# First half's recurrent phase of a decoder block: every engine's queue in program order, left operands four products ahead, recurrent gates one product later

## The chip, the cores and the metric

The kernel runs on one core of a Trainium2 chip. The metric is the device time of one execution in microseconds (us); lower is better. Times are medians of repeated runs. Engines are named as in the profile: PE (matrix multiplication), ACT (activations and copies), DVE and POOL (elementwise work), SP (which here only issues DMAs; ACT issues some too).

## What is computed

One layer of a decoder: a normalised input `h` goes through one wide projection `w_in`; its columns feed a recurrent branch, an attention branch and two merge gates.

```python
h = rms_norm(x, g_norm) * (1 + scale) + shift
x_rnn, z_rnn, q, k, v, z_attn, g_r, g_a = split(h @ w_in)      # 2048 x 1024 @ 1024 x 8192
xc = causal_depthwise_conv(x_rnn, conv_w, conv_b)              # 4 taps
r = sigmoid(blocks(xc) @ w_a + b_a); i = sigmoid(blocks(xc) @ w_x + b_x)
log_a = -8 * r * softplus(-lam); a = exp(log_a)
hr = scan(a, sqrt(1 - exp(2 * log_a)) * i * xc)                # h_t = a_t h_{t-1} + b_t
y_rnn = (hr * silu(z_rnn)) @ w_out_rnn
y_attn = (dilated_attention(rope(q), rope(k), v) * silu(z_attn)) @ w_out_attn
merged = sigmoid(g_r + b) * y_rnn + sigmoid(g_a + b) * y_attn
out = rms_norm(x + gate * (merged @ w_o), g_final)
```

All numbers are float32. A product of two float32 matrices is made of three matmuls on split operands: high times high, high times low, low times high (`mm3`). A split is one ACT copy (the high part, `hi_act`) and one POOL subtraction (the low part, `lo_pool`).

## The kernel before

The sequence of 2048 positions is worked on in two halves (`f` = 0 and 1), each of two column blocks of 512 (`j` = 0, 1). In each half the projection comes first; attention and the output products follow after both halves.

**One pair of weight tiles is seven products.** `strassen` multiplies a 2x2 arrangement of weight tiles with a 2x2 arrangement of `h` by Strassen's scheme: seven products instead of eight, each of 12 matmuls (four k-steps of `mm3`), into five PSUM tiles X, Z, W, V, Y. PE's order in a pair is X, the previous pair's last product, Z, W, V, X again, Y; the pair's own last product (into V again) is done after the next pair's X. After each product DVE or ACT adds partial results (`u1`, `u2`, `u3`) or totals a block (`total`) and hands it to `done`.

**Left operands.** The seven left operands of a pair are sums and differences of four raw weight tiles. In the first half `left_operands` makes them: four loads from HBM (`raw_tile`, a ring of five), sums on DVE (L255, L256, L258, L263) and a split of each into a tile S of a ring of seven (`split_s`: ACT L200, POOL L160). `first_operands` is a generator, so an operand is made where the program takes it for its product, and each is stored to a scratch tensor `sD` by a DMA on ACT's queue (L273). In the second half the operands are only loaded back from `sD`.

**The recurrent phase.** In each half 22 pairs come first: eight recurrent ones (`recurrent`, `m` = 0 to 7), each followed by one or two others (gates of the attention and merge branches in `gate_pairs`, plain parts of q and k in `plain_pairs`). That is 154 products. Per recurrent pair and column block, a chain of steps follows the pair's product X: `tap` (ACT), `taps` (three DVE operations, L779), `split` (ACT L154, POOL L160 into xh and xl), `gates` (six matmuls on PE into two PSUM tiles pg), `sigmoids` (ACT L792), `decay` (POOL, DVE L797), `exponentials` (ACT L802 to L804), `root` (DVE L808, ACT L809 square root), `scan` (DVE L814), `finish` and `store`. `steps_after` puts each step a number of products behind the start, and `run_late` runs it in the program after that product. The other half of a recurrent pair, `z_part`, has a sigmoid on ACT (L755) and a multiplication on POOL (L759).

**What sets the order.** In this part a scheduler does: the program gives instructions and their dependences, and the scheduler orders each engine's queue by its own estimate of when things will be ready. A few instructions are given priority (`tc.high_priority`). Once placed, an engine's queue is worked in that order on the chip: an instruction that waits holds up what stands behind it. The attention stage further on is already written under `tc.manual_schedule()`, where each engine's queue is in program order. After the recurrent phase come the rotated and the remaining plain pairs of q and k with their rotary tables (six pairs, 42 products), still in the scheduler's hands.

Of the kernel before, what the change touches and what calls it, by code (L numbers as in the profile page):

```python
# [26 lines left out]
H = 8  # L27
# [59 lines left out]
def decoder_block(ctx, tc, x, c, positions, g_norm, w_mod, b_mod, w_in, b_gate, conv_w, conv_b,  # L87
# [110 lines left out]
    def split_s(src):  # L198
        t = s_tile([P, 2, KH, P])
        last_hi[0] = nc.scalar.activation(t[:, 0], src, AF.Copy).ins  # L200
        lo_pool(t[:, 1], src, t[:, 0])
        return t

    pair_id, last_hi, last_load, last_lo, last_copy = {}, [None], [None], [None], [None]
# [3 lines left out]
    def run_late(n):  # L208
        for fn in (*late.pop(n, ()), *after_prod.pop(n, ())):
            fn()  # L210

# [14 lines left out]
    def blocks(pieces):  # L226

        cuts, tiles = [], ([], [])
# [17 lines left out]
        a11, a21, a22 = load(0, 0), load(1, 0), load(1, 1)  # L246
        return a11, load(0, 1), a21, a22

    def left_operands(pieces):

        a11, a12, a21, a22 = blocks(pieces)
        yield split_s(a11)
        s1 = T(wq, [P, KH, P], F32, "s1", bufs=1)
        s2 = T(wq, [P, KH, P], F32, "s2", bufs=1)
        nc.vector.tensor_tensor(s1[:], a21, a22, ALU.add)  # L255
        nc.vector.tensor_tensor(s2[:], s1[:], a11, ALU.subtract)  # L256
        yield split_s(s2[:])
        nc.vector.tensor_tensor(a21, a11, a21, ALU.subtract)  # L258
        yield split_s(a21)
        yield split_s(s1[:])  # L260
        yield split_s(a12)
        yield split_s(a22)
        nc.vector.tensor_tensor(s2[:], a12, s2[:], ALU.subtract)  # L263
        yield split_s(s2[:])

    def first_operands(x, pieces):

        for i, t in enumerate(left_operands(pieces)):
# [8 lines left out]
            yield t  # L277
# [41 lines left out]
    def strassen(up, f, key, pieces, done):  # L319

        x = pair_id.setdefault(key, len(pair_id))
        ops = None if f else first_operands(x, pieces)
        if f and x == 0:
            for _ in range(NS):
                load_next()

        def take():
            return (f, *loaded.pop(0)) if f else (f, 7 * x, next(ops))
# [397 lines left out]
    def reset_rows(rp, f):  # L726
        bigr = T(rp, [P, HALF], BF16, "bigr")
        for q in range(2):
            t = T(rp, [P, CH], I32, "sg", bufs=1)
# [4 lines left out]

    def recurrent(rp, bigr, f, m):
        raw = T(rp, [P, 2, P], F32, "gr_", bufs=1)
        nc.sync.dma_start(raw[:, 0, :], w_a[0, m])
        nc.sync.dma_start(raw[:, 1, :], w_x[0, m])
        gh = T(rp, [P, 2, P], F32R, "gh", bufs=1)
        gl = T(rp, [P, 2, P], F32R, "gl", bufs=1)  # L740
        hi_act(gh[:], raw[:])
        lo_pool(gl[:], raw[:], gh[:])
# [5 lines left out]
        def z_part(j, ps, u):  # L748
# [4 lines left out]
            def sigmoid():  # L753
                sg.append(T(rp, [P, CH], F32, "sg", bufs=1))
# [6 lines left out]
        def x_part(j, ps, u):  # L761
# [23 lines left out]
            def gates():  # L785
                for gt in range(2):
                    v["p", gt] = T(pg, [P, CH], F32, "pg")
                    mm3(v["p", gt][:], gh[:, gt, :], gl[:, gt, :], v["xh"][:], v["xl"][:])
# [17 lines left out]
            def root():  # L806
                t = v["t"][:]
                nc.vector.scalar_tensor_tensor(t, v["y"][:], 1.0, t, ALU.add, ALU.mult)  # L808
                nc.scalar.activation(t, t, AF.Sqrt)  # L809

            def scan():
# [3 lines left out]
                nc.scalar.activation(htail[:, m : m + 1], y[:, CH - 1 : CH], AF.Copy)  # L815

            def finish():
                z4 = zs[j][:].rearrange("p (r j) -> p r j", r=4)
# [15 lines left out]
        strassen(rp, f, ("r", m), [wcol(m * P), wcol(D + m * P)], done)  # L834
# [59 lines left out]
    def rotated_pairs(qp, f, Ct, St):  # L894

        for base, dstT, qs in QK:
# [15 lines left out]
            strassen(qp, f, (base, "rotated"), [wcol(base + hh * P, 32) for hh in range(H)], rotated)  # L912

    def plain_pairs(f):

        cuts = []
        for t in range(6):
            pieces = []
            i0 = t * P
            while i0 < (t + 1) * P:  # L920
                hd, i = divmod(i0, 96)
                n = min(96 - i, (t + 1) * P - i0)
                pieces.append((i0 - t * P, hd * P + 32 + i, n))
                i0 += n
            cuts.append(pieces)
        for base, dstT, qs in QK:
            for t in range(0, 6, 2):
                def plain(i, j, ps, u, t=t, dstT=dstT, qs=qs):
# [3 lines left out]
                    for p0, r0, m in cuts[t + i]:  # L932
                        nc.sync.dma_start(dstT[r0 : r0 + m, :, n * P : (n + 1) * P],
                                          t0[p0 : p0 + m, :].rearrange("p (r j) -> p r j", r=4))

                strassen(plain_pool[0], f, (base, t), [wcol(base + r0, n) for pc in cuts[t : t + 2] for _, r0, n in pc], plain)
                yield


    def gate_pairs(ep, f):  # L940
        for m in range(0, KT, 2):
            for base, dst, b0 in ((5 * D, zaT, None), (6 * D, grT, C_BG), (7 * D, gaT, C_BG + 8)):
                def gate(i, j, ps, u, m=m, dst=dst, b0=b0):
# [6 lines left out]
                    if b0 is None:  # L950
                        sg = T(ep, [P, CH], F32, "sg", bufs=1)
                        nc.scalar.activation(sg[:], v[:], AF.Sigmoid)
# [648 lines left out]
```

## Time and profile before

| | |
|---|---|
| median of 3 runs | 2337.65 us (2332.69 to 2343.75) |
| the profiled execution | 2338.7 us, its span 2336.9 us |
| PE busy | 2246.0 us, 96% of the span |
| DVE / ACT / POOL busy | 1347.5 / 1206.0 / 952.1 us |
| DMA | 569.21 MB, mean 244 GB/s |
| granted PE clock | 0.983 of full speed, mean |

In the profile a line number is one of the code above. Many instructions share a helper's line: all matmuls are L146, and a row names the tile written and those read (`V<-T,S`). PE is busy nearly all the time, so what can be won is the time in which it waits, and the time in which it runs at a lower clock. The stages by time from the span's start: values and set-up to 147.6 us, the first half's recurrent phase to about 641.5, its rotated and plain pairs to about 775, the second half to about 1455, attention and output after that.

### The profile page before, as it was taken

How to read it: one execution, taken by the hardware profiler on the slowest of the kernel's cores; microseconds unless marked ns; L12 is line 12 of the kernel's file. 1: busy time of each engine (PE TensorE's matmuls, PEld its weight loads, DVE VectorE, ACT ScalarE, POOL GpSimd, SP SyncE). 2: the span in 40 equal slices, each digit the busy share in tenths (PEclk: the TensorE clock that was granted, in tenths of full speed). 3: DMA queues.
4: the chain of work that ended last, by engine and by line, in shares of the span. 5: the costliest groups of instructions: out<-in, count | busy, mean ns of one | idle time of the engine just before them, and what ended most of it. 6: DMA issues, size and time to landing. Idle time of an engine off the chain costs nothing.

```text
span 2336.9 us, 34037 instructions
## 1 busy us (share of the span) xinstructions
PE 2246.0 (96%) x11461; PEld 1872.0 (80%) x11461; DVE 1347.5 (58%) x2442; ACT 1206.0 (52%) x2391; POOL 952.1 (41%) x734
## 2 busy tenths in 40 slices
PE   8998999899989999999999999999999898989998
PEld 4996777677777998787888877888889797978887
DVE  4737666756676534544434472366666777658443
ACT  4636656665643635555444411567768787634111
POOL 2456556665545533332211120446565656433000
PEclk9999999999999999999999999999999999999999
DMA  7375777676778759999677778989987887799532
GB/s 263 108 237 205 277 265 262 239 243 246 242 246 268 227 174 327 311 325 322 227 231 225 234 250 269 301 245 266 279 254 247 236 245 238 221 310 281 179 122 95
DMA packets 427284, 569.21 MB, mean 244 GB/s; under 512 B 71942, under 2 KB 292834, under 8 KB 426084
## 3 DMA queue, kind: packets, MB, share of 16 engines
q1 hardware_dynamic: 389268, 447.27, 62.2%
q10 hardware_dynamic: 37648, 119.70, 13.3%
q8 instruction: 91, 1.49, 0.3%
q14 instruction: 85, 0.70, 0.1%
q0 software_dynamic: 192, 0.05, 0.0%
HBM read 355.08 MB, written 211.82 MB: 243 GB/s over the span
## 4 chain that ended last, share of the span: by engine, by line
PE 50%; DMA 8%; DVE 4%; ACT 3%; issue 3%; POOL 2%; SPq 1%; ACTq 0%; POOLq 0%; DVEq 0%
PE pj L146 11%; PE pq L146 7%; PE X L146 6%; PE V L146 6%; PE o L146 4%; PE sc L146 4%; PE Z L146 3%; PE W L146 3%; PE Y L146 2%; PE pT L1217 1%; DMA wD<-s 1%; PE pT L1230 1%; PE pg L146 1%; DMA vraw<-vN 1%; DVE yl L163 1%
## 5 line engine op out<-in xcount | busy, mean ns | idle before, releaser
L146 PE MATMUL pj<-yh,S 128*128 128x512 f32 x1024 | 372.0, 408 | 6.1 <-DMA S<-wD 3.2
L146 PE MATMUL V<-T,S 128*128 128x512 f32 x1344 | 334.3, 397 | 12.0 <-ACT t L809 5.2
L160 POOL TENSOR_TENSOR S<-R,S 128x512 fp32r<-128x512 f32 x168 | 241.8, 1455 | 253.8 <-ACT S L200 79.2
L146 PE MATMUL X<-T,S 128*128 128x512 f32 x1344 | 332.4, 395 | 1.2 <-ACT t L888 1.2
L146 PEld LDWEIGHTS V<-T,S 128*128 128x128 f32 x1344 | 252.6, 189 | 75.9 <-ACT t L809 7.2
L146 PEld LDWEIGHTS X<-T,S 128*128 128x128 f32 x1344 | 252.4, 188 | 61.8 <-ACT t L888 2.1
L146 PEld LDWEIGHTS pj<-yh,S 128*128 128x128 f32 x1024 | 195.6, 191 | 44.0 <-DVE fg L1424 3.6
L146 PE MATMUL pj<-yl,S 128*128 128x512 f32 x512 | 203.0, 397 | 0.0
L1133 ACT ACTIVATE pp<-pp,st 128x256 f32<-128x256 f32 (+3 forms) x256 | 133.9, 524 | 113.4 <-DVE st L1132 112.7
L146 PE MATMUL W<-T,S 128*128 128x512 f32 x672 | 174.1, 404 | 0.0
L146 PE MATMUL Y<-T,S 128*128 128x512 f32 x672 | 168.6, 398 | 2.1 <-DVE t L418 2.1
L146 PE MATMUL Z<-T,S 128*128 128x512 f32 x672 | 167.4, 397 | 0.0
L146 PEld LDWEIGHTS W<-T,S 128*128 128x128 f32 x672 | 130.3, 194 | 32.4 <-issue 0.9
L146 PEld LDWEIGHTS Y<-T,S 128*128 128x128 f32 x672 | 127.0, 190 | 33.3 <-DVE t L418 2.5
L146 PEld LDWEIGHTS Z<-T,S 128*128 128x128 f32 x672 | 127.5, 190 | 30.2
L160 POOL TENSOR_TENSOR S<-s,S 128x512 fp32r<-128x512 f32 x84 | 114.9, 1369 | 77.7 <-ACT S L200 55.0
L163 DVE TENSOR_TENSOR ptl<-pT,pth 128x384 fp32r<-128x384 f32 (+1 forms) x160 | 97.8, 628 | 64.8 <-ACT pth L154 62.6
L1197 ACT ACTIVATE pp<-pp,M 128x256 f32<-128x256 f32 (+3 forms) x256 | 117.9, 523 | 8.7 <-DVE M L1321 8.6
L1132 DVE CUSTOM_DVE_ANT_0 pp<-sc,msk 128x256 f32<-128x256 f32 (+3 forms) x256 | 105.1, 449 | 30.0 <-PE sc L146 27.2
L779 DVE SCALAR_TENSOR_TENSOR xc<-xr,par,xc 128x512 f32<-128x512 f32 x96 | 84.8, 883 | 56.5 <-ACT xc L773 55.6
L160 POOL TENSOR_TENSOR kq<-kraw,kq 128x512 fp32r<-128x512 f32 (+1 forms) x64 | 101.1, 1590 | 22.9 <-ACT kq L154 22.9
L160 POOL TENSOR_TENSOR vh<-vraw,vh 128x256 fp32r<-128x256 f32 (+1 forms) x64 | 67.2, 1050 | 105.1 <-ACT vh L154 99.4
(358 smaller groups left out, 4697.7 us busy)
## 6 DMA issues: line engine op xcount, KB each, us to landing
sD<-S ACTq DMA_DIRECT2D x196, 512.0 KB, 4.2
S<-sD SPq DMA_DIRECT2D x196, 512.0 KB, 5.0
S<-wD SPq DMA_DIRECT2D x99, 512.0 KB, 5.5
R<-in_w_in_dram SPq DMA_DIRECT2D x136, 256.0 KB, 3.9
wD<-s ACTq DMA_DIRECT2D x64, 256.0 KB, 5.5
T<-in_w_mod_dram SPq DMA_DIRECT2D x8, 1024.0 KB, 11.5
vN<-ev SPq DMA_DIRECT2D x64, 128.0 KB, 2.7
zaT<-ev SPq DMA_DIRECT2D x32, 256.0 KB, 4.5
```

The lines of the kernel that those rows point to most:

```text
L146: last_mm[0] = nc.tensor.matmul(o, lhsT=l, rhs=r, start=st, stop=sp, **kw).ins
L160: nc.gpsimd.tensor_tensor(o, i, h.bitcast(F32), ALU.subtract)
L163: return nc.vector.tensor_tensor(o, i, h.bitcast(F32), ALU.subtract).ins
L779: nc.vector.scalar_tensor_tensor(xc, xr[:, i : i + CH], cw(i), xc, ALU.mult, ALU.add)
L1132: nc.vector.tensor_tensor_reduce(pdst, s_ps, mask, 1.0, 3e38, ALU.add, ALU.min, m_)
L1133: nc.scalar.activation(pdst, pdst, AF.Exp, bias=m_, scale=-1.0, accum_out=l_)
L1197: nc.scalar.activation(pp, pp, AF.Copy, scale=w)
L1217: nc.tensor.transpose(pt[:, c0 + j * P : c0 + (j + 1) * P], pp[i][:, k * P : (k + 1) * P], ident)
L1230: nc.tensor.transpose(pt[:, c * P : (c + 1) * P], pp[:, half * P : (half + 1) * P], ident)
```

## The change

1. In the first half the recurrent phase runs under `tc.manual_schedule()`: PE, DVE, ACT, POOL and SP each work in the order in which the program is written. The second half and the rotated pairs stay with the scheduler.
2. The left operands are no longer made when taken. `operand_events` lists each load, sum and split with the product that it belongs to; `pump`, called behind each product's late steps, does those that are due, LEAD = 4 products ahead of the product that uses them. Raw loads are 10 to 5 products ahead of their pair. `pair_order` gives the pairs in advance.
3. The recurrent steps from `gates` on are one product later (GATES = 5 for 4). The square root gets a step of its own, one product behind `root`'s DVE operation. The copy of `htail` moves from `scan` to `finish`. `finish` and `store` stay at 12.
4. The recurrent pair's weights `w_a`, `w_x` are loaded four products after the pair's start and split after seven.
5. Gate pairs: sigmoid one product after the total, the multiplication and the store up to two after. Plain pairs: the store one after. The tile `sg` has two buffers.

Points 3 to 5 hold in both halves.

```diff
     def run_late(n):
         for fn in (*late.pop(n, ()), *after_prod.pop(n, ())):
             fn()
+        pump()
...
+    LEAD = 4
+
+    def operand_events(x, pieces):
+        load, v = block_loads(pieces), {}
+        tt = nc.vector.tensor_tensor
...
+        def split(i, name):
+            first[7 * x + i] = t = split_s(v[name])
             kept.append((7 * x + i, t))
             if len(kept) > 2:
                 k, t2 = kept.pop(0)
-                with tc.issue_after(last_hi[0]):
-                    nc.scalar.dma_start(sD[k], t2[:].bitcast(F32))
+                nc.scalar.dma_start(sD[k], t2[:].bitcast(F32))
...
+        def sums():
+            for name in ("s1", "s2"):
+                v[name] = T(wq, [P, KH, P], F32, name, bufs=1)[:]
+            tt(v["s1"], v["a21"], v["a22"], ALU.add)
+            tt(v["s2"], v["s1"], v["a11"], ALU.subtract)
+
+        yield -6, lambda: raw("a11", 0, 0)
+        yield -5, lambda: raw("a21", 1, 0)
+        yield -4, lambda: raw("a22", 1, 1)
+        yield -1, lambda: raw("a12", 0, 1)
+        yield 0, sums
+        yield 0, lambda: split(0, "a11")
+        yield 1, lambda: tt(v["a21"], v["a11"], v["a21"], ALU.subtract)
+        yield 1, lambda: split(1, "s2")
+        yield 2, lambda: split(2, "a21")
+        yield 3, lambda: split(3, "s1")
+        yield 4, lambda: split(4, "a12")
+        yield 5, lambda: tt(v["s2"], v["a12"], v["s2"], ALU.subtract)
+        yield 5, lambda: split(5, "a22")
+        yield 6, lambda: split(6, "s2")
+
+    def pump():
+        while events and events[0][0] <= n_prod[0]:
+            events.pop(0)[2]()
...
+    GATES = 5
...
+        steps_after(n_prod[0], ((4, load_weights), (7, split_weights)))
...
             def root():
                 t = v["t"][:]
                 nc.vector.scalar_tensor_tensor(t, v["y"][:], 1.0, t, ALU.add, ALU.mult)
+
+            def square_root():
+                t = v["t"][:]
                 nc.scalar.activation(t, t, AF.Sqrt)
...
             steps_after(start[0] + 7 * j, (
-                (0, tap), (1, taps), (2, split), (4, gates), (5, sigmoids), (6, decay), (7, exponentials),
-                (9, root), (11, scan), (12, finish), (12, store)))
+                (0, tap), (1, taps), (2, split), (GATES, gates), (GATES + 1, sigmoids), (GATES + 2, decay),
+                (GATES + 3, exponentials), (GATES + 4, root), (GATES + 5, square_root), (GATES + 6, scan),
+                (GATES + 7, finish), (GATES + 7, store)))
...
+                    steps_after(n_prod[0], ((1, store),))
...
+                    steps_after(n_prod[0], ((1, sigmoid), (2, product)))
...
+    for x, (key, pieces) in enumerate(pair_order()):
+        pair_id[key] = x
+        events += [(7 * x + d - LEAD, len(events) + i, fn) for i, (d, fn) in enumerate(operand_events(x, pieces))]
+    events.sort(key=lambda e: e[:2])
...
+        pump()
         n = 0
-        for m in range(KT):
-            recurrent(rp, bigr, f, m)
-            for _ in range(1 + (m % 4 > 0)):
-                next(plain if n % 6 == 3 else gates)
-                n += 1
+        with nullcontext() if f else tc.manual_schedule():
+            for m in range(KT):
+                recurrent(rp, bigr, f, m)
+                for _ in range(others[m]):
+                    next(plain if is_plain(n) else gates)
+                    n += 1
```

What this does to the queues, at two places of the recurrent pair `m` = 1 in the first half. First ACT's queue before, around that pair's two z parts (sg), its conv input (xr, xc), its split (xh) and three left operands (S4, S5 and the store of S2, S3):

```order
L755 ACTIVATE sg_315_2148<-zs_311_2125 128x512
L815 ACTIVATE htail_96_499<-y_306_2100 128x1
L416 ACTIVATE xr_316_2150<-X_286_1995 128x512
L200 ACTIVATE S4_348_2317<-R3_326_2191 128x512
L273 DMA sD<-S2_341_2270 128x1024
L772 ACTIVATE xtail_95_498<-xr_316_2150 128x3
L773 ACTIVATE xc_317_2154<-xr_316_2150,par_2_61 128x512
L771 ACTIVATE xr_331_2230<-xtail_95_498 128x3
L200 ACTIVATE S5_354_2346<-R2_325_2189 128x512
L273 DMA sD<-S3_346_2295 128x1024
L755 ACTIVATE sg_330_2215<-zs_320_2177 128x512
L154 ACTIVATE xh_328_2211<-xc_317_2154 128x512
```

And the same stretch of ACT's queue in the change, from that pair's xc on (L806 is `tap`, L835 to L837 are `exponentials` of the pair before, L154 with S is a split of a left operand, L788 the z part's sigmoid):

```order
L806 ACTIVATE xc_326_2185<-xr_325_2181,par_2_61 128x512
L835 ACTIVATE t_329_2201<-y_317_2146 128x512
L836 ACT_TABLE_LOAD
L836 ACTIVATE a_328_2200<-y_317_2146 128x512
L837 ACTIVATE y_317_2146<-a_328_2200 128x512
L154 ACTIVATE gh_330_2205<-gr__311_2118 128x256
L154 ACTIVATE S3_332_2213<-s1_312_2123 128x512
L266 DMA sD<-S1_319_2151 128x1024
L154 ACTIVATE xh_336_2235<-xc_326_2185 128x512
L788 ACT_TABLE_LOAD
L788 ACTIVATE sg_338_2239<-zs_334_2219 128x512
L154 ACTIVATE S4_339_2241<-R3_305_2088 128x512
```

Before, the split xh stands behind both sigmoids of the z part; now it stands ahead of the second one, and S4 and S5 of the left operands come after it, although they belong to later products than before.

Second, PE's queue at the gates of that pair. Before:

```order
L146 MATMUL Z_332_2232<-T_157_1035,S1_335_2237 128x512
L146 MATMUL pg_336_2256<-xh_328_2211,gh_284_1991 128x512
L146 MATMUL pg_337_2260<-xh_328_2211,gh_284_1991 128x512
L146 MATMUL W_340_2268<-T_159_1037,S2_341_2270 128x512
L146 MATMUL W_340_2268<-T_160_1038,S2_341_2270 128x512
L146 MATMUL pg_336_2256<-xl_329_2213,gh_284_1991 128x512
L146 MATMUL pg_336_2256<-xh_328_2211,gl_285_1992 128x512
L146 MATMUL pg_337_2260<-xl_329_2213,gh_284_1991 128x512
L146 MATMUL pg_337_2260<-xh_328_2211,gl_285_1992 128x512
L146 MATMUL W_340_2268<-T_159_1037,S2_341_2270 128x512 x2
```

PE's queue at the same gates in the change:

```order
L146 MATMUL W_347_2291<-T_159_1037,S2_323_2175 128x512
L146 MATMUL pg_348_2307<-xh_336_2235,gh_330_2205 128x512
L146 MATMUL pg_348_2307<-xl_337_2237,gh_330_2205 128x512
L146 MATMUL pg_348_2307<-xh_336_2235,gl_331_2206 128x512
L146 MATMUL pg_349_2311<-xh_336_2235,gh_330_2205 128x512
L146 MATMUL pg_349_2311<-xl_337_2237,gh_330_2205 128x512
L146 MATMUL pg_349_2311<-xh_336_2235,gl_331_2206 128x512
L146 MATMUL V_354_2325<-T_155_1033,S3_332_2213 128x512
```

The gates moved from between Z and W, partly inside W, to behind the whole of W: one product later.

More of the change, by code (lines that the diff above doesn't have):

```diff
@@ L244, in load, with raw @@
             return t[:]
[L246 to L268, printed above, removed]
+        return load
+    LEAD = 4
+    def operand_events(x, pieces):
+        load, v = block_loads(pieces), {}
+        tt = nc.vector.tensor_tensor
+        def raw(name, i, half):
+            v[name] = load(i, half)
+        def split(i, name):
+            first[7 * x + i] = t = split_s(v[name])
             kept.append((7 * x + i, t))
@@ L325, in strassen @@
                 load_next()
+        n_op = iter(range(7 * x, 7 * x + 7))
         def take():
-            return (f, *loaded.pop(0)) if f else (f, 7 * x, next(ops))
+            if f:
+                return (f, *loaded.pop(0))
+            i = next(n_op)
+            return f, i, first.pop(i)
         def prod(ps, b, first, last, op=None):
```

116 lines of the change are left out of this document (72 added, 44 removed).

## The prediction

> **What bounds the kernel now.** I read the profile by stages first: which stage has PE time to give. This is the table of windows: the first half's recurrent phase, its rotated and plain pairs, and 400 us out of the second half.
>
> ```profile
> core 0: us, PE busy (x) PEld busy (x) DVE busy (x) ACT busy (x) POOL busy (x), PEclk, DMA share, GB/s
> 147.62:641.50 493.88, 464.92 (x1943) 369.13 (x1942) 328.14 (x342) 294.73 (x489) 300.00 (x211) 0.98 0.73 251
> 641.50:775.40 133.90, 124.47 (x536) 99.45 (x535) 88.24 (x148) 51.30 (x89) 72.55 (x53) 0.97 0.84 267
> 950.00:1350.00 400.00, 399.73 (x1717) 322.27 (x1716) 179.12 (x236) 196.51 (x302) 84.78 (x65) 1.00 0.81 268
> ```
>
> The second half is the yardstick: the same products with operands loaded back, and 1717 matmuls in 400 us are 0.233 us each, 2.80 per product. The first half's recurrent phase is 154 products of 12 matmuls and 16 gates of six, 1944 in all, so 452.9 us at that pace; it takes 493.9. **41.0 us are lost there.** The next 42 products would be 117.4 us, and 39 small transposes some 4.6 (four take about 0.47, an estimate from rows of four at 0.60 that overlap), so of 133.9 some 11.9 are lost there. The second half has nothing to give.
>
> Then the waits, for PE, in these two stages.
>
> ```profile
> PE pg L146 <- ACT xh L154: 17.0, 6, 5.8
> PE V L146 <- ACT t L809: 5.2, 5, 3.7
> PE V L146 <- DVE ev L418: 2.6, 1, 2.6
> PE pg L146 <- POOL xl L160: 2.1, 4, 0.5
> PE V L146 <- ACT S L200: 1.9, 1, 1.9
> ...
> PE pg L870 <- DVE rep L868: 5.8, 2, 5.0
> PE Y L146 <- DVE t L418: 2.1, 1, 2.1
> ```
>
> In the recurrent phase PE waits for 28.8 us; 22.2 of these are two kinds: gates that wait for the split xh (17.0), and products V named behind the square root (5.2). The other 12.2 of the 41.0 are not waits. The longest wait shows what they are, in PE's timeline:
>
> ```profile
> 215.79 1.56 PE L146 MATMUL Z<-T,S 128*128 128x512 f32 x6
> 223.17 1.22 PE L146 MATMUL pg<-xh,gh 128*128 128x512 f32 x2 [5.82 <-ACT xh L154]
> 225.04 0.64 PE L146 MATMUL pg<-xl,gh 128*128 128x512 f32 x1
> 226.33 0.63 PE L146 MATMUL pg<-xh,gl 128*128 128x512 f32 x1
> 230.12 2.96 PE L146 MATMUL V<-T,S 128*128 128x512 f32 x12
> 638.19 4.57 PE L146 MATMUL V<-T,S 128*128 128x512 f32 x12 [3.69 <-ACT t L809]
> ```
>
> After 5.82 us of waiting the next matmuls come 0.43 us apart for some 4 us, at half pace; after 3.69 us, twelve take 4.57 us instead of 2.96. So a long wait costs its length and some 2 to 3 us more, and the 12.2 go with the long waits.
>
> Why was xh late? ACT's timeline just before, then DVE's:
>
> ```profile
> 216.52 0.62 ACT L200 ACTIVATE S<-R 128x512 fp32r<-128x512 f32 x1
> 221.10 0.63 ACT L755 ACTIVATE sg<-zs 128x512 f32<-128x512 f32 x1 [3.96 <-DVE zs L418]
> 222.49 0.63 ACT L154 ACTIVATE xh<-xc 128x512 fp32r<-128x512 f32 x1 [0.76 <-DVE xc L779]
> 212.29 2.20 DVE L814 TENSOR_TENSOR_SCAN y<-a,htail,t 128x512 f32<-128x512 f32 x1
> 214.41 1.72 DVE L255 TENSOR_TENSOR s<-R,R 128x512 f32<-128x512 f32 x1
> 216.05 2.08 DVE L819 TENSOR_TENSOR zs<-y,zs 128x512 f32<-128x512 f32 x1
> 218.05 1.70 DVE L258 TENSOR_TENSOR R<-R,R 128x512 f32<-128x512 f32 x1
> 219.67 0.74 DVE L779 SCALAR_TENSOR_TENSOR xc<-xr,par,xc 128x512 f32<-128x512 f32 x1
> 220.33 0.68 DVE L418 TENSOR_TENSOR zs<-Y,u 128x512 f32<-128x512 f32 x1
> ```
>
> ACT stands for 3.96 us at a z part's sigmoid, whose input DVE totals only after 7.7 us of scan, sums and finish; xh stands behind that sigmoid, and PE's gates behind xh. No engine is full: in this stage DVE is busy 328.1 of 493.9 us, ACT 294.7, POOL 300.0. The loss is order, not load.
>
> **The change, part by part.** *Gates one later, xh ahead of the sigmoid that held it.* The taps come one product after X, the split two, the gates five. From the end of X that is five products, 14.0 us. The chain is xc 0.81 and ahead of it three small copies (some 1.0 together, an estimate), three taps 2.8, xh 0.63, xl 1.55:
>
> ```profile
> L773 ACT ACTIVATE xc<-xr,par 128x512 f32<-128x512 f32 x16 | 12.9, 805 | 0.0
> L779 DVE SCALAR_TENSOR_TENSOR xc<-xr,par,xc 128x512 f32<-128x512 f32 x48 | 44.3, 923 | 16.6 <-ACT xc L773 16.3
> L160 POOL TENSOR_TENSOR xl<-xc,xh 128x512 fp32r<-128x512 f32 x16 | 24.8, 1547 | 0.0
> L200 ACT ACTIVATE S<-R 128x512 fp32r<-128x512 f32 x87 | 53.2, 620 | 3.0 <-DMA qT<-ev 1.3 <-PE X L146 1.3 <-issue 0.2
> L160 POOL TENSOR_TENSOR S<-R,S 128x512 fp32r<-128x512 f32 x88 | 125.2, 1432 | 91.4 <-ACT S L200 61.4 <-issue 12.2 <-DVE ev L953 6.6
> L803 ACT ACT_TABLE_LOAD x16 | 20.5, 1283 | 0.1
> ```
>
> That makes 6.8 us, so 7.2 are left for queues. The 5.82 us wait fits into them: minus 17.0.
>
> *Operands four products ahead.* 11.2 us, of which a split needs 0.62 and 1.43. The remaining 9.1 cover any single wait of ACT in this stage (the longest at L755 is 5.8 us, row below). Minus 5.2, the wait of V. The square root, one product behind its DVE operation, adds to this cover.
>
> With both kinds the 12.2 of half pace go: 17.0 + 5.2 + 12.2 = 34.4 us. *What I keep* is the 6.6 us of the three small kinds (2.6 + 2.1 + 1.9): ordinary lateness of an eviction, an xl or a split. The lead may remove them too (minus 6.6), or a fixed order may add as many (plus 6.6).
>
> *Added work.* ACT's queue in the changed program has 12 more table loads in this stage and 13 more in the second half's. By the L803 row that is 15.4 and 16.7 us of ACT time, beside 294.7 of some 460 and 196.5 of 400 busy: off PE's path in both, price 0. Without that cover it would be all of 32 us. DVE, POOL, PE and the bytes moved stay the same.
>
> *Queues that a step is moved past.* Stores of gates, z and plain tiles now stand in SP's queue ahead of raw loads of later pairs, and wait there for DVE or ACT. A sum needs its last raw tile four products after that load's place in the program, 11.2 us; a load lands in 4.3:
>
> ```profile
> R<-in_w_in_dram SPq DMA_DIRECT2D x67, 256.0 KB, 4.3
> ```
>
> So 6.9 us are left for SP's waits: price 0. *The second half*: its gates, stores and sigmoids also move, but PE is busy 399.73 of 400 and its operands are seven tiles ahead; 0, and 3 at most. *Rotated pairs*: the scheduler orders them anew. The rotary tables now start on DVE some five products later, and PE's transposes stand after some 16 products instead of 11, so the 5.8 us wait for rep may shrink or grow; I take 0, between minus 6 and plus 6.
>
> Sum against the profiled execution: 2338.7 - 34.4 = 2304.3. That execution is 1.05 us above the median of 2337.65, so **2303 us** is forecast for the median, 1.5% less.
>
> **Rivals.** The waits of other engines that could take PE's place:
>
> ```profile
> ACT sg L755 <- DVE zs L418: 44.5, 11, 5.8
> DVE s L256 <- POOL S L160: 47.1, 19, 3.9
> DVE s L255 <- DMA R<-in_w_in_dram: 21.2, 6, 6.4
> DVE s L263 <- DMA R<-in_w_in_dram: 16.1, 8, 3.8
> ```
>
> *A, a part stays: DVE behind POOL.* The sum s2 overwrites the tile whose last split POOL does one product earlier, so in program order DVE still waits there (47.1 us, 2.5 each) with the totals of W and V behind it. PE's next use of V's bank is at least two products away, 5.6 us, so most is hidden. If a third reaches PE, 15.7 us come back: 2319.
>
> *B, no change: raw loads on a strict SP queue.* If stores hold the loads longer than the 6.9 us, DVE's waits for raw tiles (37.3 us) reach PE, since DVE can no longer do something else first: 2303 + 37 = 2340. Against it: the loads are issued up to ten products ahead of their pair.
>
> *C, slower: ACT falls behind the lead.* In three successive products ACT gets, per recurrent block with gates beside it, tanh 0.63, load 1.28, exp 0.63, square 0.62, load 1.28, sigmoid 0.63, split 0.62; split and sigmoid 1.25; load, square root, load, sigmoid and split 4.45: 11.4 us where three products take 8.4. These durations are ACT's rows L200, L803 and, for one activation, these:
>
> ```profile
> 205.78 0.63 ACT L802 ACTIVATE t<-y 128x512 f32<-128x512 f32 x1 [0.50 <-DVE y L797]
> 206.42 1.28 ACT L803 ACT_TABLE_LOAD   x1
> 207.72 0.63 ACT L803 ACTIVATE a<-y 128x512 f32<-128x512 f32 x1
> ```
>
> ACT is 3.0 us late after each such pile. If each reached PE, 16 times 3.0 and 1.6 of half pace (the 3.69 us wait: 4.57 against 2.96) would be 74 us: 2377. It decides from the point at which ACT's lateness passes the 9.1 us of the lead. Against it: ACT is idle a third of the stage, so piles do not add up.
>
> The Trainium skill (ScalarE: Activation LUTs, "What ACT_TABLE_LOAD costs") speaks against the change here: it gives some 1.28 us for a load and 1.38 for a drain, 2.66 for every switch. By that, an estimate, a pile would be 5.5 us longer, 8.5 behind, close to the whole lead, and rival C would gain. The trace does not bear it out: 207.72 - 206.42 is 1.30 us from the load's start to the next activation, and the load begins 0.64 after the tanh, so I give it no chance of its own.
>
> **How the numbers follow.** Forecast (2290 to 2312) 0.66; A (2312 to 2326) 0.14; B and other ways to no change 0.10; C 0.10. The low end is all of the 41.0 gone and 6 in the rotated pairs: 2337.65 - 47.0 = 2290.7, so 2290. The high end takes in A with the rotated pairs 6 worse: 2326. Outside are B and C, 0.2. A measurement of this kernel tells about 0.5%, 11.7 us, from no change: faster is below 2326, 0.80; within 0.10; slower 0.10.
>
> **What would show it.** In the changed profile: the recurrent phase ends some 34 us earlier; PE's waits for xh and for L809's successor are gone; matmul counts per 50 us are about 214 and the clock 1.0 from 150 to 600; ACT's waits at the z sigmoids may stay without PE behind them. The forecast is wrong if PE waits for S (C), if DVE waits for R and PE for DVE (B), if PE's waits for V behind DVE pass 10 us (A), or if the gain is lost again between the end of the phase and the second half.

## The result and the profile after

The changed kernel takes **2305.83 us**, median of 5 runs (2302.90 to 2308.77), beside 2335.00 us of the kernel before on the same chip: a ratio of 0.9857, 95% interval 0.9842 to 0.9873. The forecast was 2303 us. The profiled execution took 2306.3 us, with a span of 2304.5.

The table of windows of the kernel before, cut at the five stages that hold products: the first half's recurrent phase, its rotated and plain pairs, the second half's values, its recurrent phase, its rotated and plain pairs. The cuts are where the trace's products reach 154 and 196 in each half.

```profile
147.62:641.74 494.12, 465.16 (x1943) 369.33 (x1942) 328.38 (x342) 294.96 (x489) 300.00 (x211) 0.98 0.73 251
641.74:781.54 139.80, 130.37 (x576) 104.85 (x575) 92.19 (x153) 52.51 (x91) 76.66 (x56) 0.97 0.85 271
781.54:875.19 93.65, 93.04 (x783) 92.63 (x781) 42.29 (x78) 48.12 (x85) 37.29 (x26) 1.00 0.55 166
875.19:1331.48 456.29, 454.37 (x1944) 365.85 (x1943) 206.07 (x255) 234.19 (x365) 110.27 (x85) 1.00 0.82 274
1331.48:1456.73 125.25, 122.48 (x528) 96.61 (x527) 57.28 (x105) 18.63 (x32) 17.75 (x12) 1.00 0.83 270
```

The same five stages of the changed kernel:

```profile
147.81:599.79 451.98, 451.98 (x1949) 366.55 (x1947) 323.46 (x339) 310.60 (x496) 310.55 (x211) 1.00 0.79 271
599.79:745.04 145.25, 130.87 (x572) 103.77 (x571) 90.24 (x156) 55.79 (x95) 77.19 (x56) 0.96 0.82 268
745.04:842.28 97.24, 94.61 (x783) 94.19 (x781) 44.50 (x78) 49.95 (x87) 40.29 (x26) 0.98 0.52 155
842.28:1298.75 456.47, 452.06 (x1944) 365.11 (x1943) 198.62 (x254) 249.42 (x376) 109.32 (x85) 1.00 0.82 273
1298.75:1424.52 125.77, 122.70 (x529) 96.71 (x527) 58.32 (x107) 19.25 (x34) 17.73 (x12) 1.00 0.83 270
```

In the first row PE's busy time now equals the stage: 451.98 of 451.98 us at clock 1.00, against 465.16 of 494.12 at 0.98. The phase is 42.1 us shorter. The other rows give part of it back: 5.4 in the rotated and plain pairs, 3.6 in the second half's values, 0.2 and 0.5 after that. What follows the last product takes 880.0 us instead of 880.2, what precedes the first 0.2 more. -42.1 + 5.4 + 3.6 + 0.7 is the 32.4 us by which the span is shorter. The cut at 641.74 lies 0.9 us ahead of the end of the 154th product, 642.60; cut there, the first two figures are -43.0 and +6.3.

PE's waits in the recurrent phase (147 to 600 us) are gone; the table of waits names none. In the rotated pairs (600 to 745 us) they are these:

```profile
PE Z L146 <- ACT S L154: 4.5, 1, 4.5
PE pg L907 <- DVE rep L905: 3.5, 3, 1.3
PE X L146 <- ACT t L925: 2.1, 1, 2.1
PE X L146 <- ACT S L154: 1.9, 1, 1.9
PE V L146 <- DVE t L440: 1.4, 2, 1.1
```

The wait for rep fell from 5.8 to 3.5; four others are new or larger. That stage's order is still the scheduler's.

Now the place at which PE stood for 5.82 us before, the gates of the recurrent pair with `m` = 1. PE's timeline after, from the pair's second X product (200.75) to its gates, with the next pair's first and second X (206.34 and 221.65); then ACT's from the copy of the first of these X on:

```profile
200.75 2.96 PE L146 MATMUL X<-T,S 128*128 128x512 f32 x12
...
206.34 2.94 PE L146 MATMUL X<-T,S 128*128 128x512 f32 x12
...
217.48 0.39 PE L146 MATMUL pg<-xh,gh 128*128 128x512 f32 x1
...
221.65 2.96 PE L146 MATMUL X<-T,S 128*128 128x512 f32 x12
```

```profile
203.74 0.60 ACT L438 ACTIVATE xr<-X 128x512 f32<-128x512 f32 x1 [0.66 <-PE X L146]
...
209.23 0.61 ACT L154 ACTIVATE xh<-xc 128x512 fp32r<-128x512 f32 x1
...
211.15 0.63 ACT L788 ACTIVATE sg<-zs 128x512 f32<-128x512 f32 x1
...
215.69 0.60 ACT L373 ACTIVATE u<-X 128x512 f32<-128x512 f32 x1 [0.40 <-POOL S L160]
```

ACT copies the X of 200.75 out at 203.74, 0.03 us after its modelled end, and had waited 0.66 for it. xh follows at 209.23, ahead of the sigmoid at 211.15, and ends 7.6 us before the gates at 217.48. The copy u at 215.69 is of the next pair's first X, into whose bank PE adds at 221.65; experiment 4 comes back to it.

In the kernel before, the same X (PE's row) and its copy (ACT's row) lay much further apart:

```profile
202.75 2.96 PE L146 MATMUL X<-T,S 128*128 128x512 f32 x12
...
214.63 0.58 ACT L416 ACTIVATE xr<-X 128x512 f32<-128x512 f32 x1
```

That is 8.9 us from the end of X to the copy; a square root, a sigmoid and their table loads stood ahead of it in ACT's queue. Of the eight such copies of the phase, seven came 2.6 to 9.1 us after their X before the change; after it, none comes more than 0.9 us behind.

### The profile page after: what moved, and what is told of

Same layout as the page of the kernel before. It is cut to its first block, busy times and chain, and to the rows that moved or that the text cites. A ratio compares the mean times of both kernels' runs of the same rounds, so it can differ in the third digit from the quotient of the medians.

```text
span 2304.5 us, 34059 instructions
## 1 busy us (share of the span) xinstructions
PE 2230.6 (97%) x11461; PEld 1867.7 (81%) x11461; DVE 1333.6 (58%) x2442; ACT 1242.3 (54%) x2416; POOL 964.6 (42%) x734
## 4 chain that ended last, share of the span: by engine, by line
PE 55%; DMA 8%; DVE 4%; ACT 3%; issue 2%; SPq 2%; POOL 1%; ACTq 0%; POOLq 0%; DVEq 0%
PE pj L146 12%; PE pq L146 8%; PE X L146 8%; PE V L146 7%; PE sc L146 4%; PE o L146 4%; PE Z L146 4%; PE W L146 4%; PE Y L146 3%; DMA wD<-s 1%; PE pT L1299 1%; DMA S<-sD 1%; PE pT L1312 1%; PE pg L146 1%; DMA gaT<-ev 1%
## 5 line engine op out<-in xcount | busy, mean ns | idle before, releaser
L160 POOL TENSOR_TENSOR S<-R,S 128x512 fp32r<-128x512 f32 x168 | 251.8, 1510 | 189.6 <-ACT S L154 66.7
L160 POOL TENSOR_TENSOR S<-s,S 128x512 fp32r<-128x512 f32 x84 | 125.9, 1499 | 122.8 <-ACT S L154 96.4
L146 PE MATMUL W<-T,S 128*128 128x512 f32 x672 | 166.0, 395 | 0.3 <-POOL S L160 0.3
L812 DVE SCALAR_TENSOR_TENSOR xc<-xr,par,xc 128x512 f32<-128x512 f32 x96 | 92.6, 964 | 78.6 <-ACT xc L806 76.9
L154 ACT ACTIVATE S<-R 128x512 fp32r<-128x512 f32 x168 | 102.3, 623 | 58.6 <-DMA R<-in_w_in_dram 28.2
## 6 DMA issues: line engine op xcount, KB each, us to landing
T<-in_w_mod_dram SPq DMA_DIRECT2D x8, 1024.0 KB, 11.6
```

The costliest lines, as they stand in the source:

```text
L146: last_mm[0] = nc.tensor.matmul(o, lhsT=l, rhs=r, start=st, stop=sp, **kw).ins
L154: nc.scalar.activation(o, i, AF.Copy)
L160: nc.gpsimd.tensor_tensor(o, i, h.bitcast(F32), ALU.subtract)
L812: nc.vector.scalar_tensor_tensor(xc, xr[:, i : i + CH], cw(i), xc, ALU.mult, ALU.add)
```

## The experiments

My theory was that the lost time is order: waits caused by what stands ahead in a queue, and half pace behind the long ones. The rivals were the steps alone (lead and later gates, in whichever order) and load (ACT's added work). All kernels are the changed one with the edit shown. Stage times are read as above, from one profiled execution each; the changed kernel's own five spans lie between 2301.1 and 2307.0 us, so a stage is known to about 3 us, except where PE waits for nothing. Not tried: what points 4 and 5 of the change are worth in the first half, and which engine's queue has to be in program order.

**1. The scheduler's order, with the changed steps.**

```
-        with nullcontext() if f else tc.manual_schedule():
+        with nullcontext():
```

> The changed kernel, with the first half's recurrent phase left to the scheduler again; operands four ahead and gates five after X are kept in the code. Theory 1, the fixed order carries the gain, and the lead only makes that order workable: the scheduler puts instructions where its own model has them ready, waits of PE for xh or S come back, and at least half of the 41 us of the recurrent phase with them: 2320 to 2335 us. Theory 2, the lead and the later gates carry it, whoever sets the order: within 6 us of the changed kernel, 2300 to 2312 us, and the recurrent phase of 154 products takes 453 to 459 us. I hold theory 1 the likelier, 6 to 4.

Measured: 2362.32 us, ratio 1.0085 (1.0068 to 1.0103): 56.5 us slower than the changed kernel by the medians, 53 by the ratios, and slower than before. The recurrent phase takes 505.9 us. PE's two largest waits in it:

```profile
PE pg L146 <- ACT xh L154: 15.3, 6, 5.8
PE V L146 <- DVE ev L440: 14.7, 6, 6.3
```

The longest one for xh, in PE's timeline, and what stood ahead of xh on ACT and on DVE:

```profile
460.26 2.95 PE L146 MATMUL Y<-T,S 128*128 128x512 f32 x12
480.13 1.22 PE L146 MATMUL pg<-xh,gh 128*128 128x512 f32 x2 [5.77 <-ACT xh L154]
```

```profile
468.44 1.28 ACT L845 ACT_TABLE_LOAD   x1
469.74 0.63 ACT L845 ACTIVATE t<-t 128x512 f32<-128x512 f32 x1
470.28 0.58 ACT L438 ACTIVATE xr<-X 128x512 f32<-128x512 f32 x1
...
479.45 0.63 ACT L154 ACTIVATE xh<-xc 128x512 fp32r<-128x512 f32 x1 [0.29 <-DVE xc L812]
```

```profile
472.40 1.72 DVE L274 TENSOR_TENSOR s<-R,R 128x512 f32<-128x512 f32 x1
474.04 2.06 DVE L855 TENSOR_TENSOR zs<-y,zs 128x512 f32<-128x512 f32 x1
476.02 0.75 DVE L812 SCALAR_TENSOR_TENSOR xc<-xr,par,xc 128x512 f32<-128x512 f32 x1
```

PE ends this X where Y starts, near 460.3; ACT copies it out only at 470.28, behind a sigmoid, a square root and their table loads. In the changed kernel this step came 0.03 us after the X shown above. DVE then does a sum and a `finish` ahead of the taps. Same steps, same lead, same gates: theory 1 holds, and by more than its range (2320 to 2335); the steps alone are worth less than nothing (505.9 against 494.1 before).

**2. Gates at four, in the fixed order.**

```
-    GATES = 5
+    GATES = 4
```

> The changed kernel, with the gates of the recurrent block four products after X again, and all steps behind them one earlier; fixed order and lead are kept. From the end of X that leaves 11.2 us for a chain of 6.8 us, so 4.4 for queues. Theory 1, what held xh was the sigmoid ahead of it in ACT's queue, and the fixed order has removed that: PE's waits for xh stay under 3 us in sum, 2304 to 2310 us. Theory 2, the later gates carry it: the 17.0 us of waits for xh come back with half pace behind them, 8 to 26 us, 2314 to 2332 us. I hold theory 1 the likelier, 6 to 4.

Measured: 2315.78 us, ratio 0.9896 (0.9880 to 0.9913); the interval lies above that of the changed kernel. The phase takes 464.1 us, with these two waits ahead:

```profile
PE pg L146 <- POOL xl L160: 3.8, 5, 0.9
PE pg L146 <- ACT xh L154: 3.0, 3, 2.0
```

The time lies in theory 2's range, the waits nearer to theory 1: of the 17.0 us for xh only 3.0 return, so most were taken by the order; but one product less costs 12.1 us of phase, so the later gates are needed for the rest.

**3. Operands one and two products ahead** (the second kernel has 2 in the line shown).

```
-    LEAD = 4
+    LEAD = 1
```

> The changed kernel, with the left operands made one product ahead instead of four; fixed order and gates at five are kept. One product is 2.8 us, of which a split needs 2.05, so 0.7 us are left for queues. Theory 1, in a fixed order the lead is what covers ACT's piles (3.0 us behind after each, 16 of them): PE waits for S at each pile and at sums that DVE makes late, at least 16 times 3.0 and 1.6 of half pace, 74 us, so 2370 us or more. Theory 2, the fixed order alone does it and the lead is spare: 2300 to 2312 us. Theory 1 is the likelier, 8 to 2.

> The changed kernel, with the operands two products ahead instead of four. Two products are 5.6 us, of which a split needs 2.05, so 3.5 us are left for queues, and ACT is some 3.0 us behind after a pile. Theory 1, the cover has only to pass the pile: almost no waits of PE for S, the recurrent phase takes 452 to 458 us, 2303 to 2312 us. Theory 2, waits of several engines add up (POOL behind ACT, DVE behind POOL), so the cover has to be about three times the pile, as with four products: the phase takes 465 to 510 us, 2318 to 2365 us. With one product ahead it took 564.8 us. Even chances.

With one, 2418.28 us, ratio 1.0330 (1.0313 to 1.0347), and a phase of 564.8 us; with two, 2313.48 us, ratio 0.9896 (0.9876 to 0.9917), and a phase of 452.0. PE's waits with one product, in the phase:

```profile
PE X L146 <- POOL S L160: 32.1, 21, 3.2
PE X L146 <- ACT S L154: 31.3, 15, 2.9
```

PE waits at the first X of 21 of the 22 pairs. In the 15 where ACT is named, the split stands in ACT's queue behind the exponentials of that product and their table load; in the others POOL's half of the split is late. Two products pass it entirely: the phase is as short as with four, with no wait of PE in the table up to its end. Theory 1 holds in both for the phase; with two the total is 1.5 us over its range. (The 7 us over the changed kernel lie outside the phase: 2.2 ahead of the first product, 2.8 in the rotated pairs, 2.2 from there to the second half's last product.) So the fixed order alone does not do it: with one product of lead it is slower than the kernel before. Some lead is a condition; beyond two products, more of it gains nothing in this phase.

**4. More table loads,** four and eight ahead of each square root (the second kernel has 8 in the line shown).

```
+    pad = T(cp, [P, 1], F32, "pad")
...
             def square_root():
                 t = v["t"][:]
+                for i in range(4 if not f else 0):
+                    nc.scalar.activation(pad[:], ones[:], AF.Sigmoid if i % 2 else AF.Sqrt)
                 nc.scalar.activation(t, t, AF.Sqrt)
```

> The changed kernel, with four activations of one column ahead of each square root of the first half, two of them sigmoids, so that four more table loads stand in each of ACT's 16 piles there: 4 times 1.28 and 0.2, 5.9 us each, 95 us of ACT in all. ACT is then 8.9 us behind after each pile, against a lead that covers 9.1. Theory 1, the price of a load is 0 so long as the lateness stays under the lead: PE's waits in the recurrent phase stay under 10 us, and the time within 10 us of the changed kernel, 2300 to 2316 us. Theory 2, ACT's added work reaches PE in proportion (its sum is 295 and 41 busy already): half or more of the 95 us comes through, 2350 us or more. 7 to 3 for theory 1.

> The same with eight such activations and eight more table loads in each of the 16 piles: 11.9 us each, 190 us of ACT in all. ACT is then 14.9 us behind after each pile, 5.8 beyond the 9.1 that the lead covers. Theory 1, what is beyond the lead reaches PE, with half pace behind it: 16 times 5.8 and some 2, 125 us, so 2400 to 2460 us, and PE's waits are for S from ACT or POOL. Theory 2, ACT's idle third takes it up between the piles: under 2350 us. 7 to 3 for theory 1.

With four, 2383.86 us, ratio 1.0197 (1.0176 to 1.0219), phase 522.1 us. With eight, 2474.96 us, ratio 1.0587 (1.0566 to 1.0609), phase 615.9. In the windows of the phase ACT is busy 396.4 and 491.6 us, 85.8 and 181.0 more than in the changed kernel (the sixteenth square root falls behind its end, but its added activations ran directly behind the fifteenth, inside), and 70.1 and 163.9 us of these come through: the kernel with four loads goes as theory 2 says, the one with eight beyond the range of theory 1. And the waits are not for S at all. In the phase, with four loads and with eight:

```profile
PE X L146 <- ACT u L373: 40.4, 11, 5.6
```

```profile
PE X L146 <- ACT u L373: 125.8, 15, 12.3
```

The first of them, with four loads, on ACT and on PE:

```profile
217.16 1.28 ACT L847 ACT_TABLE_LOAD   x1
218.45 0.20 ACT L847 ACTIVATE pad<-ones 128x1 f32<-128x1 f32 x1
218.67 1.28 ACT L847 ACT_TABLE_LOAD   x1
...
224.51 0.63 ACT L848 ACTIVATE t<-t 128x512 f32<-128x512 f32 x1
...
226.09 0.58 ACT L373 ACTIVATE u<-X 128x512 f32<-128x512 f32 x1
```

```profile
206.91 2.97 PE L146 MATMUL X<-T,S 128*128 128x512 f32 x12
...
220.43 2.97 PE L146 MATMUL V<-T,S 128*128 128x512 f32 x12
226.71 5.49 PE L146 MATMUL X<-T,S 128*128 128x512 f32 x12 [3.31 <-ACT u L373]
```

The second X product of a pair adds into the bank from which ACT must first copy u1. That copy stands behind the root's pile; the lead of the operands does nothing for it. In the changed kernel u ended at 216.29 and that X began at 221.65: 5.4 us are the cover that decides here, not the 9.1 that I named. It is not the smallest: over the 22 pairs of the changed phase this margin is 3.2 to 8.0 us, least at the u of 258.24, whose X begins at 262.07. And ACT enters this pile 4.3 us later than in the changed kernel (15.9 us after the pair's X at 201.29, there 11.6 after the X at 200.75), so some lateness is carried on from the pile before; by which way is not shown, as ACT stood for 3.07 and 1.17 us in between, waiting for DVE. The rest of what came through is half pace, as in the X above, 5.49 us for 12 matmuls: PE's waits and the 2 us or so behind each.

**5. The second half's steps as before.** The late steps of the second half are put back (`steps_after` with the old lags where `f` is 1; those of the recurrent weights and of the plain stores, not shown, likewise); the first half is unchanged.

```
-                    steps_after(n_prod[0], ((1, sigmoid), (2, product)))
+                    steps_after(n_prod[0], ((0, sigmoid), (0, product)) if f else ((1, sigmoid), (2, product)))
...
+            if f:
+                steps_after(start[0] + 7 * j, (
+                    (0, tap), (1, taps), (2, split), (4, gates), (5, sigmoids), (6, decay), (7, exponentials),
+                    (9, root), (9, square_root), (11, scan), (12, finish), (12, store)))
+                return
```

> The changed kernel, with the second half's steps as they were before the change: gates four after X, root and square root together, sigmoid, product and stores of gate and plain pairs at once, recurrent weights loaded and split at the block's start. The first half is the changed one. In the changed kernel the second half lost 4.2 us that it did not lose before. Theory 1, the moved steps of the second half cost them, by waits of V and Z and by transfers that fall together: the span gets 3 to 5 us shorter, and from the marker of W at the first half's end to the first output product it takes again 666 us: 2300 to 2303 us. Theory 2, the scheduler's order there is different for another reason and such losses come and go: 2304 to 2308 us. 6 to 4 for theory 1.

Measured: 2307.40 us, ratio 0.9853 (0.9839 to 0.9868), the same as the changed kernel. The second half's recurrent phase takes 454.2 us, its rotated pairs 128.9, the values before them 95.7: theory 2. Together that is within 1 us of the changed kernel's 679.5, so the moved steps cost the second half nothing that can be measured.

**6. The fixed order through the rotated pairs.** The order is kept on until the last plain pair; angles, tables and the normalisation of x become late steps.

```
+            steps_after(n_prod[0], ((1, angles), *((d, lambda q=q, k=k: table(q, k))
+                                                   for d, q, k in ((2, 1, 0), (3, 1, 1), (4, 0, 0), (5, 0, 1)))))
...
+            steps_after(n_prod[0], ((18, lambda: norm_x(xp, x0)),))
...
+                steps_after(n_prod[0], ((0 if f else 1, finish),))
```

> The changed kernel, with the fixed order kept on through the first half's rotated and plain pairs: the rotary angles are written one product after the recurrent phase, the four tables two to five products after it, the normalisation of the next rows of x 18 products after it, and the last sum and the stores of a rotated tile one product after the rest. In the changed kernel these 42 products take 145.3 us, against 117.4 at full pace and some 4.6 for the transposes. Theory 1, what is lost there (23 us) is order as well, left to the scheduler: the stage takes 125 to 135 us, 2286 to 2297 us in all. Theory 2, it is load (raw tiles in 32-column pieces, rotary work on DVE, DMA share 0.93 and more): the stage stays within 4 us of 145, 2301 to 2311 us. Theory 3, in a fixed order PE stands at the transposes until DVE has made the tables: 150 us and more, over 2311 us. Chances 5, 3 and 2 in 10.

Measured: 2314.32 us, ratio 0.9901 (0.9884 to 0.9917); the stage takes 155.7 us. Theory 3: DVE stands for the positions and then does the whole chain of angles, and PE stands at the transposes:

```profile
610.12 0.17 DVE L882 CAST pf<-pi 128x8 f32<-128x8 int32 x1 [4.17 <-DMA pi<-in_positions_dram]
617.92 0.42 DVE L910 COPY rep<-co 128x512 f32<-128x512 f32 x1
618.40 1.12 PE L912 MATMUL pg<-cs,rep 128*128 128x128 f32 x4 [12.95 <-DVE rep L910]
```

A fixed order is only as good as the places it gives: steps written one or two products ahead of their use, behind a transfer just issued, wait in full.

**7. Angles early, rotated pairs alternating, both.** The angles become some 40 late steps of the recurrent phase, one per product (`early`); the rotated pairs take turns with the plain ones (`alternate`).

```
+        steps_after(n_prod[0], [(20 + i, fn) for i, fn in enumerate(ops)])
...
         for base, _, _ in QK:
             yield (base, "rotated"), [wcol(base + hh * P, 32) for hh in range(H)]
+            key = next(plain)
+            yield key, plain_pieces(*key)
```

> The changed kernel, with the rotary angles of each half (positions loaded, products and range reduction, some 40 small operations of 0.23 us on DVE) made during its recurrent phase, one operation per product from the twentieth on; at the start of the rotated pairs only the cosine's shift, two clamps, the sines and the four tables are left. In the changed kernel PE waits 3.5 us for rep there, in a stage of 145.3 us for the first half. Theory 1, DVE's chain of 7 us at the start of the stage holds rep and the operands behind it: 3.5 and some 2 of half pace go, the stage takes 138 to 141 us, 2299 to 2303 us in all. Theory 2, other work of DVE takes the chain's place: 143 to 147 us, 2304 to 2309 us. Even chances.

> The changed kernel, with the rotated pairs of each half alternating with the plain ones (rotated q, plain, rotated k, plain, plain) instead of two rotated in a row. With the fixed order kept on through this stage DVE took 1.77, 0.75 and 0.69 us for a rotated tile, 12.8 for the four of a pair, beside some 7 of totals and sums: 20 us, where seven products take 19.5. Theory 1, two rotated pairs in a row are more than DVE's share, and the waits of Z, X and V for S and t there (4.5, 2.1, 1.9 and 1.4 us, with half pace behind them) are that load: the stage takes 135 to 141 us, 2295 to 2303 us. Theory 2, it is the order in which the scheduler puts the splits, or the raw tiles in 32-column pieces: the stage stays at 143 to 149 us, 2303 to 2311 us. 6 to 4 for theory 1.

> Both of these edits together: angles made in the recurrent phase, rotated pairs alternating with plain ones. Theory 1, the two causes are apart, so what each saves adds up: the first half's rotated and plain pairs take 129 to 136 us, 2289 to 2297 us in all. Theory 2, one cover for both: no better than the better one of the two, within 2 us. Theory 3, neither is the cause: 143 to 149 us, 2303 to 2311 us. Chances 4, 3 and 3 in 10.

| | time, us | ratio (95%) | first half's rotated and plain | second recurrent phase |
|---|---|---|---|---|
| changed kernel | 2305.83 | 0.9857 (0.9842 to 0.9873) | 145.3 | 456.5 |
| early | 2318.29 | 0.9922 (0.9906 to 0.9938) | 144.9 | 469.0 |
| alternate | 2301.53 | 0.9851 (0.9830 to 0.9872) | 142.8 | 460.5 |
| both | 2302.26 | 0.9859 (0.9840 to 0.9877) | 133.8 | 465.2 |

Each alone leaves the stage within 3 us of where it was; both together take 11.5 us off it, more than the sum, so neither of my accounts of a single cause fits. In experiment 8, which has both, the stage is as short again, 132 us. With both, the stage is in the range of theory 1 of the third expectation (129 to 136), but the total is not, since the second recurrent phase takes 8.7 us more. The one larger wait left in the stage is again for a copy of X: X behind ACT's u, 3.8 us. With the angles early the wait for rep is gone and another has its place (600 to 760 us):

```profile
PE V L146 <- DVE t L440: 12.9, 2, 10.2
```

And the second recurrent phase, left to the scheduler, loses up to 12.5 us when its DVE gets some 40 small operations to place; with the angles early PE's longest wait there is for DVE:

```profile
1029.00 5.45 PE L146 MATMUL V<-T,S 128*128 128x512 f32 x12 [4.94 <-DVE ev L440]
```

**8. The second half's recurrent phase in the fixed order too**, on top of both edits of 7.

```
-        with nullcontext() if f else tc.manual_schedule():
+        with tc.manual_schedule():
```

> The kernel with angles early and pairs alternating, and with the fixed order for the second half's recurrent phase too; the rotated and plain pairs of both halves stay with the scheduler. Left to the scheduler, that second phase took 456.5 us in the changed kernel and 465 in the two that gave it other work (469 with the angles early), and PE's waits there were for DVE's ev and for xh and xl. Theory 1, these are the same losses as in the first half, order: the second phase takes 452 to 455 us with no waits of PE for ev or xh, and the first half stays at 134 us for its rotated pairs, 2283 to 2292 us in all, faster than the changed kernel. Theory 2, the second half's splits and stores of the output weights, placed in ACT's queue in program order, wait there for transfers and hold evictions: 460 us and more, 2293 us and more. 7 to 3 for theory 1.

Measured: **2284.99 us**, ratio 0.9757 (0.9740 to 0.9774): faster than both kernels, 1.0% below the changed one by the two ratios. The window of the second recurrent phase, then PE's waits from 825 to 1420 us, which are these two:

```profile
828.00:1281.00 453.00, 453.00 (x1948) 365.16 (x1948) 204.26 (x291) 246.02 (x371) 104.93 (x82) 1.00 0.83 271
```

```profile
PE pj L146 <- issue: 0.8, 1, 0.8
PE pg L920 <- DVE rep L918: 0.7, 1, 0.7
```

Theory 1: the phase takes 452.8 us, the pace of 0.233 us per matmul for all of its 1944, where the scheduler gave 456.5 with less to do and 465.2 with the same. The splits and stores of the output weights do not hurt in the fixed order. Little is left in hand in the first half, though: at one pair (u at 262.15) the margin between the copy u and its X has shrunk to 0.1 us.

## Why the forecast came out right

The total was right to 3 us, by two errors of opposite sign: the phase gave 42.1 us where 34.4 were forecast, and the stages behind it took back 9.7 where 0 was forecast. That these nearly cancel is luck.

- **What bounds, and the reading of half pace: right.** 41.0 us were said to be lost in the first recurrent phase; 42.1 went. The 12.2 us that were no waits went with the long waits, and the clock of the stage rose from 0.98 to 1.00. Matmul by matmul, the phase before loses 13.7 us to a pace under one per 0.233 us, all but 1.0 of it within 8 us behind a wait and 9.4 behind the four longest (5.82, 5.28, 3.86 and 3.69 us); the phase after loses none. Experiments 3 and 4 show the price anew: beyond the waits themselves, 49.0 us behind 37 short ones with one product of lead (63.8 us of waits in a phase 112.8 longer), 27.3 behind 14 with four loads (42.8 and 70.1), so 1.3 and 2.0 each; 2 to 3 had been said for long ones.
- **The terms -17.0 and -5.2: right in sum, wrongly argued.** I put them down to gates one later and to four products of lead. Experiment 1 has both and loses 53.9 us against the changed kernel. The fixed order does it; gates one later are worth 12.1 of it (experiment 2), the third and fourth product of lead nothing in the phase (experiment 3). The second product of lead is needed, but not for the V behind the square root: with one product the waits of V stay away, and X waits instead. The prediction named xh ahead of the sigmoid, which is right, but not the step ahead of that: the copy of X out of PSUM, 8.9 us late before and 9.9 in experiment 1, which the fixed order puts right behind X.
- **"What I keep", 6.6 us: this step failed.** The three small kinds of waits (V behind DVE's ev, xl, S) went too. I called them ordinary lateness of an eviction; they were order like the rest. The bound of -6.6 that I gave was the value to take.
- **Added table loads at price 0: right, with a wrong cover.** ACT is 15.6 us busier in the phase (310.60 against 294.96) and PE waits for none of it. That this is so near the forecast's 15.4 is chance: of the twelve added loads ten fall into the phase, 12.8 us. But I named the lead's 9.1 us as cover. Experiment 4 shows that u1's copy comes due first, with 3.2 us in hand at the tightest pair, and that 5.9 us more per pile already cost 70 us. So rival C was near, and at another place than the one I named.
- **SP's queue, rivals A and B: right that they cost nothing.** In the changed phase PE has no wait for V behind DVE, and DVE waits for a raw tile once, 1.6 us.
- **Rotated pairs, 0 within 6: +5.4, at the edge** (+6.3 with the cut at 642.60). I had also read the stage's end too early, at 775.4; its 42 products run to 781.4. No term of the sum hangs on that. What brings the new waits there is not shown; the stage's order is the scheduler's. Experiment 7 shows that 11.5 us can be had back, but which cause did it stays open, since the two edits help only together.
- **Second half, 0 and 3 at most: +0.7 in its products, but +3.6 in its values**, which I had left out of the sum: there PE waits 2.4 us in one place for POOL's split, and the clock of that stage is 0.98 instead of 1.00.
- **"The second half has nothing to give": wrong by 3.5 us.** The 400 us that I read as yardstick were full; the 75 us ahead of them were not. Experiment 8 takes 456.3 to 452.8.

The Trainium skill (ScalarE: Activation LUTs, "What ACT_TABLE_LOAD costs") gives a drain of some 1.38 us beside each load. Experiment 4 speaks against it again: with the extra loads, two of them begin 1.51 us apart (217.16 and 218.67), which is a load of 1.28, an activation of 0.20 and 0.03 between.

## What to carry to other kernels

Where no engine is full and the one that bounds still waits, write the order down by the products it works on, with each producer some products ahead (here two were enough and one was not): the same steps left to the scheduler were slower than before. Then ask of every engine which of its outputs comes due first; here it was the copy out of an accumulator that is soon written again, not the operands that had the lead. And fix the order stage by stage, with transfers and long chains put far ahead of their use: what is gained in one stage moves the losses in those that stay with the scheduler, by 5 to 12 us either way.

## What was not expected of the hardware

The length of a wait alone does not say whether half pace follows. In the kernel of experiment 1 two V products waited for DVE's ev almost equally long, in PE's timeline:

```profile
272.57 3.03 PE L146 MATMUL V<-T,S 128*128 128x512 f32 x12 [2.23 <-DVE ev L440]
...
407.32 4.59 PE L146 MATMUL V<-T,S 128*128 128x512 f32 x12 [2.13 <-DVE ev L440]
```

One ran its twelve matmuls at full pace in 3.03 us, the other in 4.59. What differs in the time before them was not tried.
